# S5's result turned on chip, and b's gates as two units of seven block products behind w_proj_b

## The chip, the cores and the metric

The kernel runs on one core of one Trainium2 chip. The core's engines each have their own queue of instructions: TensorE (PE in the profile; PEld is its weight load) multiplies matrices, VectorE (DVE) and ScalarE (ACT) work element by element, GpSimd (POOL) does small jobs and starts DMAs that add to their target, and SyncE (SP) starts most of the other DMAs. The metric is the device time of one execution in microseconds. Before the change it is 876.34 us, the median of three runs (876.28 to 878.51).

## The reference

One layer of a hybrid encoder for 512 tokens of width 1024, in float32. What the change touches is the first part, the two mixers and their merge:

```python
n = rms_norm(h, mix_norm_g[i])
proj = n @ w_in[i]                       # 1024 x 4608, cut by columns:
xa = proj[..., :OFF_U]                   # 512: S5's input
zu = proj[..., OFF_U:OFF_V]              # 1024
zv = proj[..., OFF_V:OFF_GA]             # 1024
gate_a = jax.nn.sigmoid(proj[..., OFF_GA:OFF_GB])    # 1024
gate_b = jax.nn.sigmoid(proj[..., OFF_GB:])          # 1024
ya = s5_branch(xa, ...)       # two scans, then y = gelu(y); y * sigmoid(y @ w_glu)
yb = sgu_branch(zu, zv, ...)  # gelu(zu) * (mixed, normalized gelu(zv))
merged = gate_a * (ya @ w_proj_a[i]) + gate_b * (yb @ w_proj_b[i])
h = h + merged @ w_out[i]
```

Behind it come a cross-attention to a memory of 256 rows (w_q, w_k, w_v, w_xo), a SwiGLU FFN of width 2816 (w_gate, w_up, w_down) and a last norm. The output is 512 x 1024.

## The kernel before, in words

**Matmuls.** Every float32 operand is split into a high part (a cast on ScalarE) and a low part (source minus high part, on VectorE); `split` (L83, its two instructions L85 and L86) does both. A product is then three matmuls, hi·hi, hi·lo and lo·hi (`mm3`, L347, the matmul L350). Activations of the mixers stand with channels on the partitions and tokens along the free dimension, so a weight block is the stationary operand and 512 tokens stream: `feat` (L352) takes 256 output columns at a time into two PSUM banks (`pf0`, `pf1`), through `feat_block` for each 512 rows of the weight, and then calls an evacuation for each 128 columns.

**Weights.** All weight blocks are in one list, `plan`, in the order of their use; each entry has loads (how many entries ahead each is to be issued) and a function that splits the loaded block. `next_w` (L322) hands out the next block, issues the loads that are due and splits up to two blocks ahead (`LOADS, SPLITS = 3, 2`). The raw blocks share three buffers. A consumer must call `next_w` in the order of the plan, which checks it. `plan_sums` (L252) hangs 32 more jobs on chosen entries: sums of blocks of w_q and w_down that later stages use (`qsum`, `dsum`, in DRAM), a copy on SyncE's queue and an accumulating DMA on GpSimd's (L268), which read the blocks of weights long before their stage.

**Seven products.** The query projection, and the FFN, compute a 2 x 2 x 2 block product with seven block products in place of eight (the Strassen-Winograd form): `product` (L1361, matmul L1370) multiplies a 512 x 256 weight block by 256 tokens, 24 matmuls of 128 x 256. Operands of some products are sums of weight blocks, or of quarters of the token matrix; the results are added in PSUM, or by ScalarE and VectorE.

**S5 on the side.** S5's work is a generator (`s5_program`, L992) that `tick` advances between the blocks of the main stream, with `later` for steps that wait for others. Its 32 groups are done in four octets. For each octet `s5_kernels` (L786) computes a small convolution kernel, spills it to DRAM (`kd`, L843 and L844 on GpSimd's queue) and loads it back eight times shifted (`tt`, L851, also GpSimd); `s5_outputs` (L942) copies the states (`ss`, L952 and L953 on ScalarE), multiplies (`py`, 48 matmuls, L966), applies gelu (L972), turns the result in four 128 x 128 transposes (`pyt`, L978), copies it (L982) and stores it to DRAM (`yd`, eight DMAs on SyncE's and ScalarE's queues). Instructions under `in_order` keep the program's order on their engine.

**Around the change.** The main stream runs: v's first half, S5's input, v's second half, a's gates (stored to DRAM, `gad`), sv, u (`zu_evac`, into `yb_hi` and `yb_lo`, in the slots E and D), and then for each 256 columns b's gates (from xn, evacuated by a sigmoid into `part`, L1155) and w_proj_b (from yb, multiplied onto `part` by VectorE, L1158). After that S5's pool is closed and a pool `merge` takes its memory: S5's result comes back from `yd` into `ygt`, is split into `yg_hi` and `yg_lo`, goes through w_glu (`glu_evac`, L1179), and w_proj_a and the merge follow (`pa_evac`, L1198), then w_out. Of the profile's stages, b's gates and w_proj_b run from about 211 to 307 us, w_glu starts at 307.6 us.

Of the kernel before, what the change touches and what calls it, by code (L numbers as in the profile page):

```python
# [17 lines left out]
P = 128  # L18
# [21 lines left out]
Q = 8  # L40
# [12 lines left out]
def hybrid_layer_kernel(  # L53
# [168 lines left out]

    def plan_units(units, down):
# [86 lines left out]
    for i in range(4):  # L310
# [7 lines left out]
    plan_sums([(5 + 3 * i, 3) for i in range(12)] + [(40 + 2 * i, 2) for i in range(8)] +  # L318
              [(79 + 3 * i, 3) for i in range(3)] + [(116 + 5 * i, 4) for i in range(9)])
# [282 lines left out]
    yd = [dp.tile([GO * C, Q, NCH], F32, name=f"yd{o}") for o in range(NO)]  # L602
# [26 lines left out]
    def s5_setup():  # L629
# [23 lines left out]
        raw_c = s5p.tile([P, 2, G, C], F32, name="raw_c")  # L653
# [94 lines left out]
        zr = s5p.tile([P, G, C], F32, name="bbr")  # L748
        zi = s5p.tile([P, G, C], F32, name="bbi")
# [192 lines left out]
    def s5_outputs(o):  # L942
# [13 lines left out]
        yt = tt.rearrange("p (i r) c -> p i r c", i=2)  # L956

        def mix_():
            ps = aux("py", (P, GO // 2, P))
            for r in range(GO // 2):  # L960
                for k in range(3):
                    for j in range(2):
                        g = 2 * r + j
                        a = (u[:, o * GO + g, :], ss[0][:, g, :], ss[1][:, g, :])[k]
                        b = (tt[:, g, :], lc(e_re, g), lc(e_im, g))[k]
                        in_order(nc.tensor.matmul(ps[64 * j:64 * j + 64, r, :], a, b, start=r == k == 0, stop=k == 2,  # L966
                                                  tile_position=(0, 64 * j), skip_group_check=True))
            later(0.5, lambda: squash(ps))

        def squash(ps):  # L970

            nc.scalar.activation(yt[:, 0], ps, AF.Gelu_apprx_tanh)  # L972
            later(1, back)

        def back():
            ps = aux("pyt", (P, GO // 2, P))
            for r in range(GO // 2):
                nc.tensor.transpose(ps[:, r, :], yt[:, 0, r, :], ident)  # L978
# [175 lines left out]
    def gb_evac(m, j, ps):  # L1154
        nc.scalar.activation(part[:, m - OFF_GB // P, :], ps, AF.Sigmoid)  # L1155

    def pb_evac(m, j, ps):
        nc.vector.tensor_tensor(part[:, m, :], ps, part[:, m, :], ALU.mult)  # L1158
# [20 lines left out]
    def glu_evac(m, j, ps):  # L1179
# [4 lines left out]
                                ygt[:, m, :].rearrange("p (l n) -> p l n", l=Q), ALU.mult)  # L1184
# [100 lines left out]
    K0, K1, T0, T1 = slice(0, 4), slice(4, 8), slice(0, 256), slice(256, 512)  # L1285
# [75 lines left out]
    def product(ps, u, q, start, ops):  # L1361

        hi, lo = next_w(u[0], u[1], q)
        for j in range(2):
            cs = slice(j * P, (j + 1) * P)
            for k in range(4):
                a = (hi[:, k, cs], lo[:, k, cs])
                b = (ops[q][0][:, k, :], ops[q][1][:, k, :])
                for i, (x, y) in enumerate(((0, 0), (0, 1), (1, 0))):
                    nc.tensor.matmul(ps[:, j, :], a[x], b[y], start=start and j == k == i == 0,  # L1370
                                     stop=k == 3 and i == 2, skip_group_check=True)
        tick(2.7)

    def unit_bank(name):
        return bank(name).rearrange("p (j t) -> p j t", j=2)

# [7 lines left out]

    def kept(x, name):
        t = np_.tile([P, 2, 256], F32, tag="ev", name=name, bufs=2)
        nc.scalar.copy(t, x)
        return t

    def minus(x, t):  # L1390
        nc.vector.tensor_tensor(t, x, t, ALU.subtract)
        return t

# [381 lines left out]
```

## Time and profile before

| what | before |
|---|---|
| median of 3 runs | 876.34 us |
| the profiled execution | 877.18 us |
| its span | 875.4 us |
| TensorE busy | 862.9 us (99%), 5753 matmuls |
| VectorE busy | 617.4 us (71%) |
| ScalarE busy | 464.1 us (53%) |
| GpSimd busy | 104.9 us (12%) |
| HBM read, written | 146.60 MB, 38.24 MB |
| the chain that ended last | TensorE 93%, VectorE 5%, ScalarE 1% |

The span is the time from the first to the last instruction of the profiled execution; the execution's own time has a little around it. A row of instructions on the timeline has start, duration, engine, line, operation, output<-inputs and shape; what stands in brackets at its end is how long the engine was idle before it, and what released it. Matmuls are pipelined, so a matmul's duration (some 0.39 us for 128 x 512) is longer than the step from its start to the next one's. A row of a stretch gives the busy time of each engine in it, the number of instructions, the granted clock of TensorE, and the share and rate of the DMA engines. In DMA groups the last number is the time from issue to landing.

### The profile page before, as it was taken

How to read it: one execution, taken by the hardware profiler on the slowest of the kernel's cores; microseconds unless marked ns; L12 is line 12 of the kernel's file. 1: busy time of each engine (PE TensorE's matmuls, PEld its weight loads, DVE VectorE, ACT ScalarE, POOL GpSimd, SP SyncE). 2: the span in 40 equal slices, each digit the busy share in tenths (PEclk: the TensorE clock that was granted, in tenths of full speed). 3: DMA queues.
4: the chain of work that ended last, by engine and by line, in shares of the span. 5: the costliest groups of instructions: out<-in, count | busy, mean ns of one | idle time of the engine just before them, and what ended most of it. 6: DMA issues, size and time to landing. Idle time of an engine off the chain costs nothing.

```text
span 875.4 us, 14560 instructions
## 1 busy us (share of the span) xinstructions
PE 862.9 (99%) x5753; PEld 759.9 (87%) x5753; DVE 617.4 (71%) x867; ACT 464.1 (53%) x684; POOL 104.9 (12%) x154
## 2 busy tenths in 40 slices
PE   9999999999999999999999999999999999999996
PEld 6787888887888888889899878999999999888875
DVE  5699679968313258669657646767877768898875
ACT  5544875277434234557557444645545454556663
POOL 1001065103311100110000001001111110000000
PEclk9999999999999999999999999999999999999998
DMA  8358369943759946825687144547788963256672
GB/s 260 112 148 249 78 200 257 248 125 107 205 133 278 263 134 211 270 88 174 196 262 218 52 137 128 145 129 187 178 217 212 233 165 79 82 166 198 194 249 87
DMA packets 112134, 154.34 MB, mean 176 GB/s; under 512 B 13545, under 2 KB 78593, under 8 KB 112002
## 3 DMA queue, kind: packets, MB, share of 16 engines
q1 hardware_dynamic: 93042, 128.27, 45.2%
q0 software_dynamic: 16432, 24.09, 16.6%
q10 hardware_dynamic: 2592, 1.05, 0.5%
q8 instruction: 45, 0.74, 0.3%
q14 instruction: 23, 0.19, 0.1%
HBM read 146.60 MB, written 38.24 MB: 211 GB/s over the span
## 4 chain that ended last, share of the span: by engine, by line
PE 93%; DVE 5%; ACT 1%; issue 1%; POOL 0%; POOLq 0%
PE pf L350 29%; PE pt L350 17%; PE px L1370 12%; PE dx L350 7%; PE pq L1370 6%; PE dq L350 3%; PE pv L1370 3%; PE qx L1370 2%; PE dv L350 2%; PE ptr L511 1%; PE py L966 1%; PE po L350 1%; PE qq L1370 1%; DVE wlo L86 1%; PE pz L902 1%; PE pw L883 1%
## 5 line engine op out<-in xcount | busy, mean ns | idle before, releaser
L86 DVE TENSOR_TENSOR wlo<-wraw,whi 128x1024 fp32r<-128x1024 f32 (+1 forms) x139 | 165.0, 1187 | 110.2 <-ACT whi L85 106.9
L85 ACT CAST whi<-wraw 128x1024 fp32r<-128x1024 f32 (+1 forms) x139 | 142.3, 1024 | 168.2 <-PE pf L350 60.1
L350 PE MATMUL pf<-xn,whi 128*128 128x512 f32 x448 | 140.6, 393 | 0.0
L350 PEld LDWEIGHTS pf<-xn,whi 128*128 128x128 f32 x448 | 83.4, 188 | 17.9 <-issue 1.1
L350 PE MATMUL pf<-xn,wlo 128*128 128x512 f32 x224 | 87.7, 391 | 0.0
L1370 PE MATMUL px<-fn,whi 128*128 128x256 f32 x480 | 83.3, 277 | 0.0
L1370 PEld LDWEIGHTS px<-fn,whi 128*128 128x128 f32 x480 | 72.4, 188 | 0.3 <-ACT u L1630 0.2
L85 ACT CAST whi<-b 128x1024 fp32r<-128x1024 f32 x40 | 42.1, 1053 | 50.5 <-PE px L1370 27.1
L86 DVE TENSOR_TENSOR wlo<-b,whi 128x1024 fp32r<-128x1024 f32 x40 | 49.0, 1224 | 28.0 <-ACT whi L85 28.0
L1370 PE MATMUL px<-fn,wlo 128*128 128x256 f32 x240 | 66.5, 277 | 0.0
L350 PE MATMUL dx<-whi,s 128*128 128x512 f32 x170 | 53.9, 392 | 1.4 <-ACT whi L85 1.0
L1370 PE MATMUL pq<-s,whi 128*128 128x256 f32 x320 | 55.1, 277 | 0.0
L86 DVE TENSOR_TENSOR wlo<-t,whi 128x1024 fp32r<-128x1024 f32 x30 | 36.7, 1225 | 20.1 <-ACT whi L85 20.1
L85 ACT CAST whi<-t 128x1024 fp32r<-128x1024 f32 x30 | 31.6, 1052 | 36.0 <-PE pv L1370 12.6
L350 PEld LDWEIGHTS pf<-xn,wlo 128*128 128x128 f32 x224 | 42.1, 188 | 8.6
L1370 PEld LDWEIGHTS pq<-s,whi 128*128 128x128 f32 x320 | 48.3, 188 | 0.1
L1370 PEld LDWEIGHTS px<-fn,wlo 128*128 128x128 f32 x240 | 45.1, 188 | 0.0
L1370 PE MATMUL pq<-s,wlo 128*128 128x256 f32 x160 | 44.3, 277 | 0.0
L350 PE MATMUL pt<-whi,xn 128*128 128x512 f32 x128 | 42.4, 404 | 0.0
L350 PEld LDWEIGHTS dx<-whi,s 128*128 128x128 f32 x170 | 31.7, 188 | 8.4 <-ACT whi L85 1.2
L350 PE MATMUL dx<-wlo,s 128*128 128x512 f32 x85 | 33.1, 390 | 0.0
L1370 PEld LDWEIGHTS pq<-s,wlo 128*128 128x128 f32 x160 | 30.1, 188 | 0.0
(436 smaller groups left out, 2132.1 us busy)
## 6 DMA issues: line engine op xcount, KB each, us to landing
wraw<-in_w_in_dram SPq DMA_DIRECT2D x36, 512.0 KB, 5.2
dsum<-in_w_down_dram SPq DMA_DIRECT2D x20, 512.0 KB, 6.9
wraw<-dsum SPq DMA_DIRECT2D x20, 512.0 KB, 4.1
b<-in_w_gate_dram SPq DMA_DIRECT2D x15, 512.0 KB, 4.1
b<-in_w_up_dram SPq DMA_DIRECT2D x15, 512.0 KB, 3.9
wraw<-in_w_down_dram SPq DMA_DIRECT2D x15, 512.0 KB, 3.8
dsum<-in_w_down_dram POOLq DMA_DIRECT2D x10, 512.0 KB, 7.6
dsum<-dsum POOLq DMA_DIRECT2D x10, 512.0 KB, 7.7
```

The costliest lines, as they stand in the source:

```text
L85: hi = nc.scalar.copy(dst_hi, src)
L86: lo = nc.vector.tensor_tensor(dst_lo, src, dst_hi.bitcast(F32), ALU.subtract)
L350: nc.tensor.matmul(ps, a[x], b[y], start=start and i == 0, stop=stop and i == 2, skip_group_check=free)
L511: tr = nc.tensor.transpose(ps[:, j, :], src[:, k * P:(k + 1) * P], ident)
L883: nc.tensor.transpose(ps[:, j, :], wt[:, 4 * hf + j, :], ident)
L902: in_order(nc.tensor.matmul(ps[hf, g, :], wt[:, g, hf], x, start=g == 0, stop=True, tile_position=(0, 64 * j), skip_group_check=True))
L966: in_order(nc.tensor.matmul(ps[64 * j:64 * j + 64, r, :], a, b, start=r == k == 0, stop=k == 2, tile_position=(0, 64 * j), skip_group_chec ...
L1370: nc.tensor.matmul(ps[:, j, :], a[x], b[y], start=start and j == k == i == 0, stop=k == 3 and i == 2, skip_group_check=True)
```

## The change

S5's result no longer goes through DRAM. Its four transposes become sixteen 64 x 64 matmuls with an identity per octet, which leave the result in PSUM with the layout that w_glu reads; one copy brings it into `ygt` (two tiles of the "gain" buffers). The DMAs to and from `yd` are gone.

w_proj_b now runs through as a whole first, evacuated by a plain copy on ScalarE. b's gates come after it, as two units of 512 columns with seven block products each, in the overlapping order `ORDER`. Their token quarters are the rows of xn itself, left in place; three sums of quarters are made on VectorE during w_proj_b (`gate_sum`), and split into the slots D and E once yb is done with. Weight sums are made by accumulating DMAs on GpSimd and on VectorE, in a tile of S5's pool. The results go through a sigmoid on ScalarE and are multiplied onto `part` on VectorE. `product`, `unit_bank`, `kept` and `minus` are the functions that the query projection had; they only move up. The places of the jobs of `plan_sums` are adapted to the shorter plan. After the change mm3's matmul is L390 and product's L1210.

```diff
+    GATES = [(w_in, OFF_GB), (w_in, OFF_GB + 512)]
+    ORDER = ((1, 0), (2, 0), (5, 0), (6, 0), (1, 1), (7, 0), (2, 1), (5, 1), (6, 1), (3, 0), (7, 1), (4, 0), (4, 1), (3, 1))
+    def plan_gates():
+        kh = KD // 2
+        for q, i in ORDER:
...
+            def make(q=q, i=i, b=b, got=got):
+                t, b11 = (gate_place[0](2 * i + j) for j in range(2))
+                if q in (2, 3):
+                    return halves(got.pop("raw"))
+                ops = halves(b11 if q in (1, 7) else t)
+                if q == 5:
+                    nc.vector.tensor_tensor(t, t, got.pop("raw"), ALU.add)
+                elif q == 6:
+                    nc.vector.tensor_tensor(b11, t, b11, ALU.subtract)
+                    nc.gpsimd.dma_start(t, b(1, 0), accum_op=ALU.add)
+                return ops
+            loads = {1: [(5, whole(2 * i + 1, b(0, 0)))], 2: [(LOADS, plain(b(1, 0)))],
+                     5: [(8, whole(2 * i, b(0, 0))),
+                         (6, lambda i=i, b=b: nc.gpsimd.dma_start(gate_place[0](2 * i), b(0, 1), accum_op=ALU.add)),
+                         (LOADS, plain(b(1, 1)))],
+                     3: [(LOADS, plain(b(1, 1)))]}
...
     for c0 in range(0, D, 256):
-        plan_feat(w_in, OFF_GB + c0, KD)
         plan_feat(w_proj_b, c0, KD)
+    plan_gates()
...
-    plan_sums([(5 + 3 * i, 3) for i in range(12)] + [(40 + 2 * i, 2) for i in range(8)] +
-              [(79 + 3 * i, 3) for i in range(3)] + [(116 + 5 * i, 4) for i in range(9)])
+    plan_sums([(5 + 3 * i, 3) for i in range(10)] + [(38, 5), (44, 5)] + [(50 + 2 * i, 2) for i in range(7)] +
+              [(85 + 3 * i, 3) for i in range(3)] + [(122 + 5 * i, 4) for i in range(10)])
...
-            nc.scalar.activation(yt[:, 0], ps, AF.Gelu_apprx_tanh)
+            nc.scalar.activation(yl.rearrange("p l (r c) -> p r l c", c=C), ps.rearrange("p r (l c) -> p r l c", c=C),
+                                 AF.Gelu_apprx_tanh)
             later(1, back)
 
         def back():
-            ps = aux("pyt", (P, GO // 2, P))
-            for r in range(GO // 2):
-                nc.tensor.transpose(ps[:, r, :], yt[:, 0, r, :], ident)
+            ps = aux("pyt", (P, Q, NCH))
+            for l in range(Q):
+                for j in range(2):
+                    hf = slice(64 * j, 64 * j + 64)
+                    in_order(nc.tensor.matmul(ps[hf, l, :], yl[hf, l, :], ident[hf, hf], start=l == 0, stop=True,
+                                              tile_position=(64 * j, 64 * j), skip_group_check=True))
             later(0.5, lambda: emit(ps))
 
         def emit(ps):
-            nc.scalar.copy(yt[:, 1], ps)
-            y = yt[:, 1].rearrange("p r (g n) -> p (r g) n", n=NCH)
-            ydo = yd[o].rearrange("(g c) l n -> l c g n", c=C)
-            for l in range(Q):
-                (nc.sync, nc.scalar)[l % 2].dma_start(ydo[l], y[C * l:C * l + C])
+            if o % 2 == 0:
+                ygt.append(np_.tile([P, 2, T], F32, tag="gain", name="ygt", bufs=2))
+            nc.scalar.copy(ygt[o // 2][:, o % 2, :], ps.rearrange("p l n -> p (l n)"))
...
-    def gb_evac(m, j, ps):
-        nc.scalar.activation(part[:, m - OFF_GB // P, :], ps, AF.Sigmoid)
-
     def pb_evac(m, j, ps):
-        nc.vector.tensor_tensor(part[:, m, :], ps, part[:, m, :], ALU.mult)
-
-    for c0 in range(0, D, 256):
-        feat(w_in, OFF_GB + c0, xn, KD, gb_evac)
+        nc.scalar.copy(part[:, m, :], ps)
...
+    gate_place[0] = gate_tile
+    for n, c0 in enumerate(range(0, D, 256)):
         feat(w_proj_b, c0, yb, KD, pb_evac)
+        gate_sum(n)
+
+    gd, ge = (slot(tag, (P, KD * T), F32R, "gs" + tag.lower()) for tag in "DE")
+    at_ = lambda t, i: t[:, i:i + 1024].rearrange("p (k n) -> p k n", k=4)
+    gops[5], gops[6] = halves_at(gd, 4, 256, APART), halves_at(ge, 4, 256, APART)
+    gops[3] = (at_(gd, 2176 + APART[0]), at_(ge, 2048 + APART[1]))
+    split(*gops[5], gsum[1])
+    split(*gops[6], gsum[2])
+    onto(gsum[2], gops[2], ALU.add)
+    split(*gops[3], gsum[2])
...
+    def gate_put(i, f, ts, src):
+        m = 4 * i + 2 * f
+        V.tensor_tensor(part[:, m:m + 2, ts], part[:, m:m + 2, ts], src, ALU.mult)
...
+    def gate_step(q, i):
+        u = GATES[i]
+        if q == 1:
+            gx[i], gv[i] = unit_bank("gx"), unit_bank("gv")
+            product(gx[i], u, 1, True, gops)
+            nc.scalar.copy(gv[i], gx[i])
+        elif q == 2:
+            product(gv[i], u, 2, False, gops)
+            gate_put(i, 0, T0, sigmoid(gv[i]))
+        elif q == 5:
+            gq[i] = unit_bank("gq") if i == 0 else aux("gq").rearrange("p (j t) -> p j t", j=2)
+            product(gq[i], u, 5, True, gops)
+        elif q == 6:
+            product(gx[i], u, 6, False, gops)
+            nc.scalar.copy(u2s[i], gx[i])
+        elif q == 7:
+            product(gx[i], u, 7, False, gops)
+            u3 = minus(gq[i], kept(gx[i], "u3"))
+            gate_put(i, 1, T1, sigmoid(u3, u3))
+        elif q == 4:
+            product(gx[i], u, 4, False, gops)
+            gate_put(i, 0, T1, sigmoid(gx[i]))
+        else:
+            product(gq[i], u, 3, False, gops)
+            u2 = minus(gq[i], u2s[i])
+            gate_put(i, 1, T0, sigmoid(u2, u2))
+
+    for q, i in ORDER:
+        gate_step(q, i)
     finish_side()
     s5.close()
...
-    ygt = mgp.tile([P, 4, T], F32, name="ygt")
     for m in range(4):
-        nc.sync.dma_start(ygt[:, m, :], yd[m].rearrange("p l n -> p (l n)"))
-        split(yg_hi[:, m, :], yg_lo[:, m, :], ygt[:, m, :])
+        split(yg_hi[:, m, :], yg_lo[:, m, :], ygt[m // 2][:, m % 2, :])
```

More of the change, by code (lines that the diff above doesn't have):

```diff
@@ L601, in hybrid_layer_kernel @@
     ud = dp.tile([SW, Q, NCH], F32, name="ud")
-    yd = [dp.tile([GO * C, Q, NCH], F32, name=f"yd{o}") for o in range(NO)]
+    ygt = []
     st = {}
@@ L747, in s5_setup @@
         yield 1.5
[L748 to L749 removed]
+        zr = s5p.tile([P, G, C], F32, tag="bbr", name="bbr")
+        zi = s5p.tile([P, G, C], F32, tag="bbi", name="bbi")
         w = s5p.tile([P, 2, G, C], F32, tag="etmp", name="bbw")
@@ new lines, in product @@
+    def product(ps, u, q, start, ops):
+        hi, lo = next_w(u[0], u[1], q)
+        for j in range(2):
+            cs = slice(j * P, (j + 1) * P)
+            for k in range(4):
+                a = (hi[:, k, cs], lo[:, k, cs])
+                b = (ops[q][0][:, k, :], ops[q][1][:, k, :])
+                for i, (x, y) in enumerate(((0, 0), (0, 1), (1, 0))):
+                    nc.tensor.matmul(ps[:, j, :], a[x], b[y], start=start and j == k == i == 0,
+                                     stop=k == 3 and i == 2, skip_group_check=True)
+        tick(2.7)
@@ L1359, in values @@
             split(ot_hi[:, 2 * hd + dt_, :], ot_lo[:, 2 * hd + dt_, :], ps)
[L1361 to L1375, printed above, removed]
     def query_product(ps, n, q, start=False):
@@ L1383, in seed @@
         return v
[L1385 to L1392, printed above, removed]
     pts = {}
```

69 lines of the change are left out of this document (64 added, 5 removed).

## The prediction

> **What bounds the kernel now.** I read the page's busy shares, then its chain, then busy time by stretch, then single matmuls on the timeline.
>
> ```profile
> span 875.4 us, 14560 instructions
> PE 862.9 (99%) x5753; PEld 759.9 (87%) x5753; DVE 617.4 (71%) x867; ACT 464.1 (53%) x684; POOL 104.9 (12%) x154
> PE 93%; DVE 5%; ACT 1%; issue 1%; POOL 0%; POOLq 0%
> ```
>
> ```profile
> core 0: us, PE busy (x) PEld busy (x) DVE busy (x) ACT busy (x) POOL busy (x), PEclk, DMA share, GB/s
> 211.30:259.50 48.20, 48.20 (x343) 39.41 (x342) 16.63 (x19) 23.64 (x25) 17.99 (x34) 1.00 0.62 159
> 259.50:307.40 47.90, 47.90 (x215) 39.73 (x214) 16.78 (x18) 14.55 (x18) 5.61 (x6) 1.00 0.91 258
> 307.40:330.00 22.60, 22.60 (x101) 18.73 (x100) 12.91 (x15) 8.68 (x12) 1.17 (x1) 1.00 0.42 116
> 486.00:490.00 4.00, 3.41 (x25) 2.87 (x24) 4.00 (x16) 4.00 (x17) 0.00 (x0) 1.00 0.26 91
> ```
>
> TensorE carries 93% of the chain. The changed stage is the first two stretches (b's gates and w_proj_b, with S5's last octets between) and the third is w_glu and w_proj_a behind it: TensorE is busy in every microsecond of them. So whatever shortens TensorE's stream there shortens the kernel, one for one, and whatever makes TensorE wait lengthens it. VectorE and ScalarE are under half busy in the first two: there the order of their work counts, not the amount. For the same reason the 32 stores and four loads of S5's round trip through DRAM, which go, earn nothing: no wait of TensorE in these rows hangs on them.
>
> **The pace of TensorE.** Start to start, on the timeline (start, duration, engine, line):
>
> ```profile
> 224.48 0.40 PE L350 MATMUL pf<-yb_hi,whi 128*128 128x512 f32 x1
> 233.79 0.39 PE L350 MATMUL pf<-yb_hi,wlo 128*128 128x512 f32 x1
> 436.62 0.39 PE L1370 MATMUL qq<-hse,whi 128*128 128x256 f32 x2
> 439.34 0.39 PE L1370 MATMUL qv<-hn,whi 128*128 128x256 f32 x2
> 556.42 0.40 PE L1370 MATMUL pv<-fn,whi 128*128 128x256 f32 x2
> 558.54 0.63 PE L350 MATMUL pf<-fn,s 128*128 128x256 f32 x4
> ```
>
> Between the first two rows lie 41 intervals: 9.31 us, 0.2271 us for a 128x512 matmul. Between the third and the fourth lie the 24 matmuls of one block product: 2.72 us, 0.1133 us for a 128x256 one, half of the wide one. The last two show a second pace: 18 narrow matmuls in 2.12 us, 0.1178 us.
>
> **Term 1, the gates' matmuls.** Before: two halves of 512 columns, each 8 token-and-weight blocks, together 192 matmuls of 128x512: 192 x 0.2271 = 43.6 us. After: 2 units x 7 products x 24 = 336 of 128x256: 336 x 0.1133 = 38.1 us. That is -5.5 us. At the slower pace it would be 39.6 us and -4.0. I take -5.5, since the new units stand in one unbroken run, as the query products of the third row do, with all of S5's small matmuls ahead of them. w_proj_b's own 192 matmuls and S5's products stay the same in number.
>
> **What one wait costs.**
>
> ```profile
> 505.20 0.39 PE L350 MATMUL po<-p_hi,vt 128*128 128x512 f32 x1
> 506.26 0.50 PE L350 MATMUL pt<-whi,ot_hi 128*128 128x512 f32 x1 [0.68 <-ACT ot_hi L85]
> 506.60 0.40 PE L350 MATMUL pt<-wlo,ot_hi 128*128 128x512 f32 x1
> 307.35 0.39 PE L350 MATMUL pf<-yb_hi,wlo 128*128 128x512 f32 x1
> 307.58 0.39 PE L350 MATMUL pf<-yg_hi,whi 128*128 128x512 f32 x1
> ```
>
> From 505.20 to 506.60 is 1.40 us where two steps take 0.45: 0.95 us lost for 0.68 us shown idle. So a wait costs its idle time and about 0.26 us. The last two rows are the place where the gates' stage ends now: w_glu follows w_proj_b at the ordinary step, without a wait.
>
> The operations of ScalarE (ACT) and VectorE (DVE) that the waits below are made of:
>
> ```profile
> L85 ACT CAST whi<-b 128x1024 fp32r<-128x1024 f32 x40 | 42.1, 1053 | 50.5 <-PE px L1370 27.1
> L86 DVE TENSOR_TENSOR wlo<-b,whi 128x1024 fp32r<-128x1024 f32 x40 | 49.0, 1224 | 28.0 <-ACT whi L85 28.0
> L1155 ACT ACTIVATE part<-pf x8: 590/596/601, 222.2 to 297.6; 128x512 f32<-128x512 f32 x8
> L1158 DVE TENSOR_TENSOR part<-pf,part x8: 683/692/692, 232.9 to 307.8; 128x512 f32<-128x512 f32 x8
> L85 ACT CAST yg_hi<-ygt x4: 620/620/622, 273.8 to 279.9; 128x512 fp32r<-128x512 f32 x4
> L1382 ACT COPY qv<-qx x2: 578/578/578, 437.7 to 448.5; 128x512 f32<-128x512 f32 x2
> ```
>
> **Term 2, into the gates.** The token sums of products 5 and 6 go into the slots that held yb, so their splits (ScalarE hi, VectorE lo) can begin only when w_proj_b's last matmul has read yb. TensorE meanwhile has product 1 of the first unit: 24 x 0.1133 = 2.72 us. ScalarE in its order: sum hi 1.05, weight hi 1.05, the last copy of w_proj_b 0.58, second sum hi 1.05, the seed copy of a product 0.58. VectorE: sum lo 1.22 from 1.08 on, then the weight's lo 1.22: done at 3.5. Product 5 has issued its two hi matmuls by 2.9 and waits for that: 0.6 us. Product 6 then needs five VectorE passes in a row: the second sum's lo, which can start at 3.8 when ScalarE has cast its hi, a weight addition, an addition to the next token sum, a weight subtraction and the weight's lo, each 1.22: done at 9.9. TensorE, with products 5 and 2 behind it and the first 0.6 us lost, is there at 9.3: 0.6 more. Those two waits are the term: +1.2 us, from +0.3 (they overlap with TensorE's queue and only one restart is paid) to +1.9 (both with 0.26 us). Behind them each operand is ready 0.2 to 1 us early by the same adding up; if one more is late it is by less than the 1.22 us of one VectorE pass.
>
> **Term 3, out of the gates.** Now nothing can follow at once: w_glu's operand yg lies in memory that S5's pool gives back, and its first ScalarE cast waits for the last gate multiply, which reads a tile of that pool. From T, the end of the last product: VectorE's subtraction 0.69 (the multiply's 692 ns row is the same shape), ScalarE's sigmoid 0.60. But ScalarE has begun the cast of a w_proj_a block at T - 0.1 (1.05, so the sigmoid starts at about T + 0.97), and VectorE has its lo half (1.22) ahead of the gate multiply: that runs from T + 0.97 to 2.2. The multiply ends at T + 2.9, yg's first cast (0.62) at T + 3.6. With 0.26 us of restart: +3.9 us. Without the block's split between, 0.69 + 0.60 + 0.69 + 0.62 = 2.6 and 0.26: 2.9 is the lower end; 5.1, one more VectorE pass ahead, the upper. The cover that this wait takes away is w_proj_b: its 192 matmuls stood there, and they have gone ahead of the gates. After it, w_glu's remaining operands follow at 0.62 and 0.69 us each, against 12 matmuls (2.7 us) per block, so nothing else is late; w_glu's own weights are split before T.
>
> **Term 4, turning S5's result.**
>
> ```profile
> 259.51 0.60 PE L978 MATMUL pyt<-ident,tt 128*128 128x128 f32 x4
> 259.87 0.47 PE L350 MATMUL pf<-yb_hi,whi 128*128 128x512 f32 x1
> 91.24 2.08 PE L902 MATMUL pz<-u,wsx 128*64 128x64 f32 x64
> 93.25 0.44 PE L883 MATMUL pw<-ident,inx 128*128 128x128 f32 x2
> ```
>
> Four full transposes (0.36 us) become sixteen 64x64 matmuls per octet. The nearest row is pz, 64 of 64 columns in 2.01 us, 0.031 each: 0.50 us per octet. +0.14 x 4 = +0.5 us; ends -0.4 (two halves of the array at once) and +1.2. The copy out of PSUM stays on ScalarE; the 16 DMA issues on its queue and 16 on SyncE's go, at no gain for TensorE, which waited for neither.
>
> **Term 5, GpSimd's queue.** Four accumulating gate loads join it, among kd's stores and tt's loads for S5, and the w_down sums are placed anew.
>
> ```profile
> 236.28 0.51 POOL L844 DMA_DIRECT2D kd<-ks x1 [2.89 <-DMA dsum<-in_w_down_dram]
> 236.79 1.20 POOL L268 DMA_DIRECT2D dsum<-in_w_down_dram  x1
> 238.87 0.56 POOL L851 DMA_DIRECT2D tt<-kd  x1 [0.87 <-PE pf L350]
> 243.32 0.53 POOL L851 DMA_DIRECT2D tt<-kd  x1 [0.56 <-DMA dsum<-in_w_down_dram]
> 251.62 0.44 PE L966 MATMUL py<-tt,u 128*64 128x128 f32 x4
> tt<-kd POOLq DMA_DIRECT2D x16, 64.0 KB, 4.2
> dsum<-in_w_down_dram POOLq DMA_DIRECT2D x2, 512.0 KB, 6.8
> ```
>
> A transfer here already waits for an accumulate eight places before it to land (the 2.89 and 0.56). Octet 3's last tt load issues at 243.3, lands at some 247.5, and TensorE reads it at 251.6: 4 us of slack. Two accumulates more ahead of it, each 1.2 us to issue and 6.8 to land, one of them waited for, take 2.4 to 8 of those 4 us while w_proj_b's stream moves the reading some 2 us later. By adding up, it is ready 1 us before it is read, plus or minus 3. I take 0, with ends 0 and +4. The sums' SyncE halves only wait for free tiles, and the second unit's last accumulate lands 28.3 to 31.8 us behind the gates' start where it is needed by 30.4: 0, at most +1.4.
>
> **Sum.** -5.5 + 1.2 + 3.9 + 0.5 + 0 = +0.1 us. The profiled execution took 877.18 us (span 875.4), 0.84 above the median of 876.34 and within the runs shown (876.28 to 878.51). Forecast: 877.3 us, no change within 0.3% (2.6 us, which is also about the least that this measurement can tell from none). Terms 1 to 3 are both sure in sign and close to each other in size, so the outcome lies with the small ones.
>
> **Rivals.**
> - Faster. The two entry waits vanish behind TensorE's queue (0.3) and the exit costs its lower end (2.9), with term 4 at nothing: -5.5 + 0.3 + 2.9 - 0.4 = -2.7, and 0.6 less where w_proj_a's cast, now ahead of the sigmoid, runs earlier than T - 0.1: 873.9 us. For it: ScalarE and VectorE are under half busy in the first two stretches. Against: the operations in each chain are in a fixed order, and each of them needs the one before.
> - Slower by S5's octet. GpSimd's queue makes tt late, and TensorE, whose order is fixed, waits ahead of py: 3 to 4 us, 880.8. For it: the 2.89 us wait above; against: 4 us of slack now. It decides when tt's last load lands over 1 us later than I add up.
> - Slower by pace. After the waits the gates and the matmuls behind go at 0.1178 and 0.2333 instead: 336 x 0.0045 = 1.5 us, and as much in w_glu, w_proj_a and w_out: 880.3. For it: the 556.42 rows; against: the query products.
> - Slower by the clock. The exit would be TensorE's longest wait since its start; if it came back at half speed for about as long as it had waited, fifteen wide matmuls (3.4 us) would take 0.227 us more each: +3.4, 880.7. Against: the granted clock is 1.00 in every row above, the one with 0.59 us idle too; no row has an idle time of 3 us. The Trainium skill (TensorE: Matmul & The Clock Gate, "What's actually happening") has the clock halved after a whole idle window of some 3.4 us, of free-running phase. By that rule a 3.6 us idle stretch would seldom hold a whole window, so the sum would mostly stay at 877.3; an estimate from the page, one such window spent at half speed, would add 1.7 us and make it 879.0. The rows above agree as far as they go, with waits under 1 us at a granted clock of 1.00; no run so far shows a wait that long.
>
> **How the numbers follow.** The sum as it stands: 0.42, with 875.0 to 879.6 as its own range. Faster: 0.20. S5's octet 0.18, pace 0.12, clock 0.08. That gives faster 0.20, same 0.42, slower 0.38. The range for 8 in 10 goes from 872.8 (terms 2 to 4 at their low ends, -2.7, and the exit's 2.9 reduced to its last three operations, 1.9 us, with w_proj_a's split and the subtraction out of the way, -1.0 and -0.7) to 881.8 (octet case with part of the pace).
>
> **What would show it.** In the new profile: 336 narrow L1210 matmuls at 0.1133 in one run; two idles of about 0.6 us in its first 10 us, released by VectorE's lo; one idle of about 3.6 us ahead of the first pf<-yg_hi, released by ScalarE's cast of yg_hi; sixteen pyt matmuls in 0.5 us; py without a wait. I am wrong if the idle ahead of w_glu is under 2 us, if py shows a wait over 1 us on tt, if the granted clock drops behind the exit, or if a wait appears in w_proj_a or later.

## The result, and the profile after

The changed kernel takes 892.67 us against 876.34 us before: 1.8% longer, ratio 1.0179, 95% interval 1.016 to 1.0199. The prediction said 877.3 us, with 872.8 to 881.8 as its range.

The page of the changed kernel, busy time and chain:

```profile
span 891.9 us, 15074 instructions
PE 867.3 (97%) x6009; PEld 769.6 (86%) x6009; DVE 647.3 (73%) x895; ACT 476.6 (53%) x704; POOL 110.5 (12%) x158
PE 87%; DMA 5%; DVE 4%; issue 2%; ACT 2%; SPq 0%; POOLq 0%; POOL 0%; DVEq 0%; ACTq 0%
```

TensorE is busy 4.4 us longer though it has less arithmetic, and the chain now has 5% of DMA, which it did not have at all. To see how much belongs to the changed stretch, I take two marks that both kernels have: one of S5's products (`py`) shortly ahead of the first new instruction, and w_out's first matmul. Before, then after:

```profile
192.62 0.55 PE L966 MATMUL py<-e,ss 128*64 128x128 f32 x6
340.22 0.39 PE L350 MATMUL pt<-whi,mg_hi 128*128 128x512 f32 x1
```

```profile
193.24 0.44 PE L1006 MATMUL py<-e,ss 128*64 128x128 f32 x4
356.32 0.39 PE L390 MATMUL pt<-whi,mg_hi 128*128 128x512 f32 x1
```

147.60 us have become 163.08: 15.5 of the 16.3 us lie between these marks. All runs below are read by this stretch. Of what is in it, the waits come first (from the changed kernel's list of TensorE's waits: who waited, for whom, total, times, longest), and then stretches around the two long ones (busy time by engine, granted clock, DMA):

```profile
PE py L1006 <- DMA tt<-kd: 4.6, 1, 4.6
PE pf L390 <- ACT yg_hi L85: 3.6, 1, 3.6
PE pk L858 <- DVE e L847: 1.1, 1, 1.1
...
243.00:251.00 8.00, 5.45 (x49) 5.28 (x50) 4.29 (x4) 0.21 (x1) 4.73 (x8) 0.57 1.01 224
251.00:256.00 5.00, 5.00 (x24) 3.84 (x24) 1.11 (x1) 1.44 (x2) 2.92 (x6) 1.00 0.21 49
316.00:319.40 3.40, 0.00 (x0) 0.00 (x0) 2.41 (x4) 2.00 (x4) 0.14 (x1) 0.90 0.50 160
319.40:326.00 6.60, 6.59 (x17) 5.17 (x17) 2.48 (x4) 1.51 (x3) 1.16 (x1) 0.54 0.91 317
```

Both waits are followed by a stretch in which the granted clock is at half: 0.57 and 0.54 as means, 0.50 microsecond by microsecond. So a wait is paid twice, as idle time and as slow matmuls behind it. The first sits ahead of S5's third octet, the second between the gates and w_glu. GpSimd's timeline ahead of the first one:

```profile
223.42 1.35 POOL L258 DMA_DIRECT2D gw<-in_w_in_dram  x1 [8.15 <-DMA gw<-in_w_in_dram]
226.26 1.18 POOL L308 DMA_DIRECT2D dsum<-in_w_down_dram  x1 [1.49 <-DMA dsum<-in_w_down_dram]
226.99 1.02 POOL L891 DMA_DIRECT2D tt<-kd  x1
229.16 1.30 POOL L258 DMA_DIRECT2D gw<-in_w_in_dram  x1 [1.15 <-DMA gw<-in_w_in_dram]
237.99 1.04 POOL L891 DMA_DIRECT2D tt<-kd  x2 [2.91 <-DMA dsum<-in_w_down_dram]
```

The first gate accumulate (L258) waits 8.15 us for the block that it adds to, and the loads of `tt` stand behind it; the last two of them issue from 238.0 us on, where `py` wants its data at 240.8. The small matmuls of the turning, on TensorE's timeline:

```profile
201.47 1.15 PE L1022 MATMUL pyt<-ident,tt 64*64 64x64 f32 x32
203.70 0.43 PE L858 MATMUL pk<-e,bd 128*32 128x128 f32 x8 [1.09 <-DVE e L847]
272.00 1.15 PE L1022 MATMUL pyt<-ident,tt 64*64 64x64 f32 x32
273.08 0.50 PE L390 MATMUL pf<-yb_lo,whi 128*128 128x512 f32 x1
```

An octet's turning occupies 1.08 us where four transposes took 0.36: sixteen matmuls of the program stand as 32 in the trace. And the gates themselves:

```profile
275.71 0.40 PE L1210 MATMUL gx<-xn,whi 128*128 128x256 f32 x2
299.32 0.28 PE L1210 MATMUL gx<-gse,wlo 128*128 128x256 f32 x1
301.81 0.28 PE L1210 MATMUL gq<-gsd,wlo 128*128 128x256 f32 x1
304.31 0.39 PE L1210 MATMUL gx<-xn,whi 128*128 128x256 f32 x2
312.93 0.29 PE L1210 MATMUL gq<-gsd,whi 128*128 128x256 f32 x1
315.56 0.28 PE L1210 MATMUL gq<-gsd,wlo 128*128 128x256 f32 x1
319.41 1.65 PE L390 MATMUL pf<-yg_hi,whi 128*128 128x512 f32 x3 [3.58 <-ACT yg_hi L85]
```

From 275.71 to 315.67 are 39.96 us for the 336 matmuls: 3.6 less than 43.6, not 5.5. From 304.31, 72 matmuls that stream xn take 8.62 us, 0.1197 each; from 299.32, 22 that stream a split sum take 2.49, 0.1132 each.

### The profile page after: what moved, and what is told of

Read it like the earlier page. It is cut to its first block, busy times and chain, and to the rows that moved or that the text cites. A ratio compares the mean times of both kernels' runs of the same rounds, so it can differ in the third digit from the quotient of the medians.

```text
span 891.9 us, 15074 instructions
## 1 busy us (share of the span) xinstructions
PE 867.3 (97%) x6009; PEld 769.6 (86%) x6009; DVE 647.3 (73%) x895; ACT 476.6 (53%) x704; POOL 110.5 (12%) x158
## 4 chain that ended last, share of the span: by engine, by line
PE 87%; DMA 5%; DVE 4%; issue 2%; ACT 2%; SPq 0%; POOLq 0%; POOL 0%; DVEq 0%; ACTq 0%
PE pf L390 20%; PE pt L390 17%; PE px L1210 12%; PE dx L390 6%; PE pq L1210 6%; PE dq L390 3%; PE pv L1210 3%; PE qx L1210 2%; DMA dsum<-in_w_down_dram 2%; PE gx L1210 2%; PE dv L390 2%; DVE wlo L86 1%; PE po L390 1%; PE qq L1210 1%; PE py L1006 1%
## 5 line engine op out<-in xcount | busy, mean ns | idle before, releaser
L86 DVE TENSOR_TENSOR wlo<-wraw,whi 128x1024 fp32r<-128x1024 f32 (+1 forms) x135 | 160.0, 1186 | 93.3 <-ACT whi L85 93.0
L85 ACT CAST whi<-wraw 128x1024 fp32r<-128x1024 f32 (+1 forms) x135 | 138.0, 1023 | 141.8 <-PE pf L390 39.3
L390 PE MATMUL pf<-xn,whi 128*128 128x512 f32 x320 | 100.2, 393 | 0.0
L1210 PE MATMUL px<-fn,whi 128*128 128x256 f32 x480 | 83.3, 276 | 0.0
L1210 PEld LDWEIGHTS px<-fn,whi 128*128 128x128 f32 x480 | 72.6, 188 | 0.3 <-ACT u L1763 0.2
L390 PEld LDWEIGHTS pf<-xn,whi 128*128 128x128 f32 x320 | 59.6, 188 | 12.8 <-issue 0.7
L1210 PE MATMUL px<-fn,wlo 128*128 128x256 f32 x240 | 66.4, 277 | 0.0
L390 PE MATMUL pf<-xn,wlo 128*128 128x512 f32 x160 | 62.6, 392 | 0.0
L390 PE MATMUL dx<-whi,s 128*128 128x512 f32 x170 | 53.9, 391 | 1.4 <-ACT whi L85 1.0
L1210 PE MATMUL pq<-s,whi 128*128 128x256 f32 x320 | 55.2, 276 | 0.0
L1210 PEld LDWEIGHTS pq<-s,whi 128*128 128x128 f32 x320 | 48.4, 188 | 0.1
L1210 PEld LDWEIGHTS px<-fn,wlo 128*128 128x128 f32 x240 | 45.1, 188 | 0.0
L390 PE MATMUL pt<-whi,xn 128*128 128x512 f32 x128 | 43.7, 416 | 0.7 <-ACT xn L85 0.7
L1210 PE MATMUL pq<-s,wlo 128*128 128x256 f32 x160 | 44.2, 277 | 0.0
L390 PEld LDWEIGHTS dx<-whi,s 128*128 128x128 f32 x170 | 31.7, 188 | 8.4 <-ACT whi L85 1.2
L390 PEld LDWEIGHTS pf<-xn,wlo 128*128 128x128 f32 x160 | 30.1, 188 | 6.3 <-issue 0.2
L390 PE MATMUL dx<-wlo,s 128*128 128x512 f32 x85 | 33.2, 391 | 0.1
L1210 PEld LDWEIGHTS pq<-s,wlo 128*128 128x128 f32 x160 | 30.1, 188 | 0.0
```

Of the source, the lines that this page charges most:

```text
L85: hi = nc.scalar.copy(dst_hi, src)
L86: lo = nc.vector.tensor_tensor(dst_lo, src, dst_hi.bitcast(F32), ALU.subtract)
L390: nc.tensor.matmul(ps, a[x], b[y], start=start and i == 0, stop=stop and i == 2, skip_group_check=free)
```

## The experiments

The theory from the traces has four parts: GpSimd's queue (the first wait and its half clock), the way out of the gates (the second), the turning, and the pace of the products on xn. Each was first taken away or done alone, then the remedies were put together. "Stretch" is the time between the two marks; the ratios are to the kernel before, run beside it.

**The clock behind the exit.** An addition of unread matmuls:

```diff
     for q, i in ORDER:
         gate_step(q, i)
+    p = aux("long")
+    for i in range(16):
+        in_order(nc.tensor.matmul(p, xn_hi[:, 0, 0:P], xn_hi[:, 0, :], start=True, stop=True))
     finish_side()
```

> The changed kernel with sixteen 128x512 matmuls on xn, whose result nobody reads, between the last gate product and w_glu. Changed kernel 892.7 us. Theory (the wait of 3.58 us ahead of w_glu also halves the clock behind it): the sixteen take 16 x 0.227 = 3.6 us in the place of the wait, the granted clock stays at 1.00, and the first fifteen w_glu matmuls go at 0.227 and not 0.43: 2.7 us less, 890.0. Rival (the slow matmuls there wait for yg's splits or for DMA traffic): they stay at 0.43, 892.7.

Measured: 889.56 us, ratio 1.0132 (1.0117 to 1.0148); stretch 159.67, 3.4 us less. TensorE's timeline at the place, and the stretch behind it:

```profile
314.16 3.80 PE L1327 MATMUL long<-xn 128*128 128x512 f32 x16
317.91 0.96 PE L390 MATMUL pf<-yg_hi,whi 128*128 128x512 f32 x3
317.90:325.00 7.10, 7.10 (x32) 5.90 (x32) 2.49 (x4) 1.53 (x3) 1.11 (x1) 1.00 0.88 308
```

With the same data coming at the same time, w_glu runs at a clock of 1.00: 32 matmuls in 7.1 us, where the changed kernel has 17 in 6.6. The slow matmuls were neither yg's splits nor the DMA traffic (0.88 here too), and the half clock costs some 3 us at this wait: w_glu's 48 matmuls take 11.0 us instead of 13.8. Most of the rest of the 3.4 us lies at the first wait, whose half clock lasted 3.4 us in this run and 6.8 in the changed kernel's.

**The w_down sums in GpSimd's queue.**

```diff
-    plan_sums([(5 + 3 * i, 3) for i in range(10)] + [(38, 5), (44, 5)] + [(50 + 2 * i, 2) for i in range(7)] +
+    plan_sums([(5 + 3 * i, 3) for i in range(8)] + [(50 + 2 * i, 2) for i in range(7)] + [(64 + 4 * i, 3) for i in range(4)] +
```

> The changed kernel with the four w_down sums whose accumulating DMAs stand in GpSimd's queue among S5's last octets placed some 20 to 30 blocks later. Theory (those sums hold up the tt loads, TensorE waits 4.56 us ahead of py, and comes back at half clock): the wait and the half clock go, 4.56 + 0.26 + 2.4 = 7.2 us less, 885.5. Rival (the gate's own accumulating loads hold tt up as well): py still waits some 2 to 4 us and the time falls by under 3 us, to 890 or more.

Measured: 890.7 us, ratio 1.0140 (1.0123 to 1.0157); stretch 160.95, 2.1 us less. The rival held: a wait of 3.5 us stays, with its half clock. Of the 2.1 us only 1.1 are this wait; 1.3 are the exit, where the half clock lasted 3.4 us in this run and not 6.8. GpSimd's timeline shows why the wait stays, since the gate accumulates wait as before and `tt`'s last load comes at 234.4:

```profile
221.35 1.35 POOL L258 DMA_DIRECT2D gw<-in_w_in_dram  x1 [7.91 <-DMA gw<-in_w_in_dram]
225.79 1.30 POOL L258 DMA_DIRECT2D gw<-in_w_in_dram  x1 [3.10 <-DMA gw<-in_w_in_dram]
234.44 0.53 POOL L891 DMA_DIRECT2D tt<-kd  x1 [2.79 <-DMA gw<-in_w_in_dram]
```

The list of waits names a store of `kd` for this wait; but GpSimd's next issue, at 239.45, is released by `tt`'s landing, and `py` starts at 239.47. The order of TensorE's work changes with the edit, too: `py` stands 14 wide matmuls (3.2 us) further ahead in it, and 16 in the two runs below that take the gate sums off GpSimd's queue, so it asks for `tt` earlier.

**yg split within the gates.** yg, ya and a's gates go into dead tiles of S5's pool (`Pair` holds two of them):

```diff
-    for q, i in ORDER:
...
+    for n, (q, i) in enumerate(ORDER):
         gate_step(q, i)
-    finish_side()
-    s5.close()
...
+        if n == 10:
+            finish_side()
+            yg_hi, yg_lo = s5p.tile([P, 4, T], F32R, tag="u", name="yg_hi"), Pair("tt", "yg_lo")
+            for m in range(4):
+                split(yg_hi[:, m, :], yg_lo[:, m, :], ygt[m // 2][:, m % 2, :])
+    ya_hi, ya_lo = Pair("e0", "ya_hi"), Pair("e1", "ya_lo")
...
     for c0 in range(0, D, 256):
         feat(w_proj_a, c0, (ya_hi, ya_lo), 4, pa_evac)
-    mgx.close()
+    s5.close()
```

> The changed kernel with yg, ya and a's gates in dead tiles of S5's pool, so that the pool is given back after w_proj_a and yg is split behind the eleventh of the fourteen gate products. Theory (the wait ahead of w_glu is the chain subtraction, sigmoid, multiply and cast, and nothing else): no wait there, no half clock: 3.58 + 0.26 + 2.7 = 6.5 us less, 886.1. Rival (ScalarE and VectorE have no room for yg's eight passes of 0.6 to 0.7 us within the gates): the waits move into the last gate products, and less than half of it is gained, 889.5 or more.

Measured: 885.28 us, ratio 1.0082 (1.0062 to 1.0102); stretch 155.59, 7.5 us less. The exit of the gates on its timeline:

```profile
315.44 0.28 PE L1210 MATMUL gq<-gsd,wlo 128*128 128x256 f32 x1
315.55 0.40 PE L390 MATMUL pf<-yg_hi,whi 128*128 128x512 f32 x1
```

The last product and w_glu follow each other at the ordinary step. The wait, its restart and its half clock were the chain of subtraction, sigmoid, multiply and cast behind a pool that was given back late; the eight passes for yg find room among the last products. With it goes a wait of 0.54 us in w_proj_a, on VectorE's `mg`.

**Where xn lies.**

```diff
-    xn_hi, xn_lo = token_slot("xn")
+    xn_hi, xn_lo = token_slot("xn", APART)
```

> The changed kernel with xn's two halves shifted by 48 and 112 elements in their slot, as the query's and the FFN's operands are. Theory (the gate products that stream xn go at 0.1196 and not 0.1133 because of where xn lies): 8 of 14 products, 192 x 0.0063 = 1.2 us less, 891.5, and gx<-xn at 0.1133. Rival (the slower pace comes from what runs before): no change, 892.7, xn products at 0.1196.

Measured: 892.53 us, ratio 1.0165 (1.0150 to 1.0180), so no gain that can be told from the changed kernel's 1.0179. The timeline of the three last xn products:

```profile
303.77 0.50 PE L1210 MATMUL gx<-xn,whi 128*128 128x256 f32 x3
311.93 0.28 PE L1210 MATMUL gq<-gsd,whi 128*128 128x256 f32 x1
```

They do go at 8.16 us for 72, 0.1133 each, so the place of the operand mattered here; but the first product on xn went at 0.1178 in the same run. What the gates win the wide matmuls on xn lose: ahead of the first mark, the longest unbroken run (96 of pf<-xn) takes 22.57 us from its start to the next work's instead of 21.94, and all runs of 15 or more 2.6 us more together. The stretch is 160.57, 2.5 us less, of which the gates are 1.1; 0.8 are a shorter wait ahead of `pk`, and 1.0 the first wait's half clock, which lasted 3.4 us in this run and not 6.8.

**The gate sums off GpSimd's queue.** A plain load and one addition on VectorE:

```diff
+                elif q == 1:
+                    nc.vector.tensor_tensor(t, t, got.pop("raw"), ALU.add)
...
-            loads = {1: [(5, whole(2 * i + 1, b(0, 0)))], 2: [(LOADS, plain(b(1, 0)))],
+            loads = {1: [(5, whole(2 * i + 1, b(0, 0))), (LOADS, plain(b(0, 1)))], 2: [(LOADS, plain(b(1, 0)))],
                      5: [(8, whole(2 * i, b(0, 0))),
-                         (6, lambda i=i, b=b: nc.gpsimd.dma_start(gate_place[0](2 * i), b(0, 1), accum_op=ALU.add)),
```

> The changed kernel with the first sum of each gate unit (two weight blocks for product 5) made by a plain load and one VectorE addition, in place of the accumulating DMA on GpSimd's queue; the w_down sums stay where they are. Changed kernel 892.7 us. Theory (the two gate accumulates wait in GpSimd's queue for whole blocks to land, and tt's loads stand behind them): the first tt load of octet 2 issues some 8 us earlier, py waits under 1 us and the half clock behind it goes, 5 to 7 us less, 886 to 888. Rival (the w_down sum between kd's stores and tt's loads is enough to hold tt): py still waits 2 us or more, above 889.

Measured: 886.82 us, ratio 1.0099 (1.0082 to 1.0116); stretch 157.10, 6.0 us less. The wait ahead of `py` falls to 1.3 us (the profile names no releaser for it), and the clock stays at 1.00 there. That the first load of `tt` would issue some 8 us earlier did not come: it issues at 226.37, since a w_down sum now holds the queue, on GpSimd's timeline:

```profile
225.64 1.19 POOL L309 DMA_DIRECT2D dsum<-in_w_down_dram  x1 [11.16 <-DMA dsum<-in_w_down_dram]
226.37 4.14 POOL L892 DMA_DIRECT2D tt<-kd  x7
233.86 0.53 POOL L892 DMA_DIRECT2D tt<-kd  x1 [3.35 <-DMA dsum<-in_w_down_dram]
```

**Both off the queue.** The edits of the last run and of the one on the w_down sums together.

> The gate sums by VectorE and the four w_down sums placed later, together. Theory (these two are all that holds tt up): no wait ahead of py, 4.56 + 0.26 + 2.4 = 7.2 us less than the changed kernel, 885.5. Rival (kd's stores or the octet's own products are late too): a wait of over 1 us stays, above 887.

Measured: 887.28 us, ratio 1.0110 (1.0095 to 1.0125); stretch 155.98, 7.1 us less, and `py` follows without a wait. On GpSimd's timeline `tt`'s first load is 11 us earlier than in the two runs where one of the causes is still there:

```profile
215.27 4.22 POOL L892 DMA_DIRECT2D tt<-kd  x8 [1.53 <-DMA kd<-ks]
```

The stretch agrees with the 7.2 expected. In the whole time the 1.1 us gained over the last run do not show: behind the second mark the profiled execution is 3.6 us longer than the last run's, with four new waits of 0.3 to 0.8 us at the query projection and ahead of it. That the sums placed there bring them is not shown; "all four" below has the sums in the same places and none of these waits.

**The turning alone**, in the kernel before: only the diff's part from `yl` to `emit`, and `ygt`.

> The kernel before with S5's result turned on chip, and nothing else of the change: b's gates and w_proj_b as they were. Theory of the traces (the sixteen 64x64 matmuls of an octet take 1.07 us where four transposes took 0.36, and the third octet's kernel products then wait 1.1 us for VectorE): 4 x 0.71 + 1.1 + 0.26 = 4.2 us more than before; without that wait, which depends on the order around it, 2.8. The prediction's term: 0.5 more. Rival (the DMAs saved give it back in less traffic): no change.

Measured: 880.2 us, ratio 1.0032 (1.0019 to 1.0045); stretch 151.64 against 147.60, 4.0 us more. Its timeline:

```profile
200.02 1.15 PE L982 MATMUL pyt<-ident,tt 64*64 64x64 f32 x32
202.28 0.42 PE L818 MATMUL pk<-e,bd 128*32 128x128 f32 x8 [1.11 <-DVE e L807]
```

4 x 0.71 + 1.1 + 0.26 = 4.2 was the theory's sum. The prediction's 0.5 falls, and so does the notion that fewer DMAs give it back.

**All four edits.**

> The changed kernel with all four edits: yg early, gate sums by VectorE, w_down sums later, xn shifted. If the losses add up: 892.7 - 6.5 (or the 7.4 measured for yg early) - 7.2 - 1.2 = 877 to 878, as long as the kernel before and up to 1 us more, with the turning's 4 us as what eats the gates' 5.5. Rival (they overlap, the DMA queues or VectorE become the limit): above 880.

Measured: 879.87 us, ratio 1.0028 (1.0017 to 1.0039); stretch 148.38. By the ratios 1.5 of the 1.8% are back; it is not as fast as before. The gates' timeline held a surprise:

```profile
296.81 0.40 PE L1211 MATMUL gx<-xn,whi 128*128 128x256 f32 x2
305.29 0.28 PE L1211 MATMUL gq<-gsd,whi 128*128 128x256 f32 x1
```

The same 72 xn products that took 8.16 us with xn shifted alone take 8.48 here, 0.1178 each, and so do all others of these gates. The place of xn is the same; so the pace has a second cause, which these runs do not name.

**The gates without the turning.** The edits for yg, the gate sums and the w_down sums, with the transposes and the way through `yd` as before:

```diff
...
+            for m in range(4):
+                if m % 2 == 0:
+                    ygt.append(np_.tile([P, 2, T], F32, tag="gain", name="ygt", bufs=2))
+                nc.sync.dma_start(ygt[m // 2][:, m % 2, :], yd[m].rearrange("p l n -> p (l n)"))
```

> The gates' seven products and w_proj_b ahead of them, with yg early, gate sums by VectorE and the w_down sums later, but S5's result turned by four transposes and taken through DRAM as before; xn where it was. Theory (the turning costs 3 to 4 us on TensorE's path, the gates gain 5.5 less 1.2 to 2 of pace and 0.5 of waits): 879.9 - 3.5 = 876.4 against 877.3 of before, up to 2 us faster than before. Rival (the loads from DRAM come too late for yg, or the sixteen-fold stores hold up weights): a wait ahead of w_glu, 879 or more.

Measured: 880.03 us, ratio 1.0033 (1.0018 to 1.0047); stretch 149.19. Neither expectation held: w_glu has its operands in time, but TensorE waits twice at the gates' entry. Its waits, and ScalarE's timeline there:

```profile
PE gx L1209 <- ACT whi L85: 1.7, 2, 1.6
PE gq L1209 <- ACT whi L85: 1.5, 1, 1.5
```

```profile
262.70 1.82 ACTq L1028 DMA_DIRECT2D yd<-tt  x4
264.56 0.59 ACT L1197 COPY part<-pf 128x512 f32<-128x512 f32 x1 [1.89 <-DMA yd<-tt]
```

The last octet's four stores on ScalarE's queue hold it for 1.9 us, while it has to make the gates' first splits; the run on the stores below tests this. In the kernel before, TensorE did not wait for ScalarE there. So the turning does bring something: not the DMAs' traffic, but ScalarE's queue.

**One wide matmul ahead of product 5**, in that kernel: `long_idle(xn_hi)` for the first unit.

> The same with one 128x512 matmul that nobody reads ahead of product 5 of the first unit. Theory (the pace of the narrow products is a state that one wide matmul or a wait sets back): the gates go at 0.1133 where their operands allow it, 0.5 to 1.5 us less than without it. Rival (the pace is fixed by where the operands lie): no change, or 0.2 us more.

Measured: 881.37 us, ratio 1.0034 (1.0021 to 1.0048); stretch 149.77. The rival held: every product behind it has the pace that it had without (72 of gx<-xn in 8.62 us). What sets the pace is not set back by a wide matmul.

**The shift in that kernel.**

> The kernel of the first of these three with xn shifted by 48 and 112 elements. Theory (the shift speeds the gates' narrow products on xn by up to 1.2 us and slows the wide matmuls on xn of the stages ahead by about as much, as the run with the shift alone showed: octet 1's product began 1.2 us later there): no change within 0.5 us. Rival (only the gates are touched): 1.2 us less.

Measured: 883.02 us, ratio 1.0055 (1.0036 to 1.0075); stretch 149.61. No gain: a wait of 1.56 us at the entry is followed here by 3.4 us of half clock (granted clock 0.50 from 273 to 275), the shifted gates then go at 0.1178, and the wide matmuls on xn ahead of the first mark lose 2.6 us as in the other run with the shift, more than the 1.2 us expected. The mark comes at 194.21 instead of 191.40, but without the shift it lies anywhere from 191.36 to 193.35.

**The stores off ScalarE's queue.**

```diff
-                (nc.sync, nc.scalar)[l % 2].dma_start(ydo[l], y[C * l:C * l + C])
+                nc.sync.dma_start(ydo[l], y[C * l:C * l + C])
```

> The gates' seven products without the turning (the kernel of three runs ago: yg early, gate sums by VectorE, w_down sums later, S5's result through DRAM), with all eight stores of an octet on SyncE's queue, none on ScalarE's. Theory (the four stores of the last octet hold ScalarE up for 3.7 us just ahead of the gates, and TensorE waits 3.2 us for the weights' casts): the two waits of 1.5 us go, 880.0 - 3 = 877, as long as before or up to 1 us less. Rival (SyncE's queue is held up by twice as many stores and the weights' loads behind them are late): a wait on DMA appears, 879 or more.

Measured: 877.86 us against 878.75 beside it (medians), ratio 0.9997 (0.9985 to 1.0009, which covers the 0.9990 of the medians); stretch 145.75. The two waits are gone, and this version is as fast as the kernel before. Its gates, from their first matmul to w_glu's:

```profile
263.15 0.40 PE L1209 MATMUL gx<-xn,whi 128*128 128x256 f32 x2
304.16 0.40 PE L391 MATMUL pf<-yg_hi,whi 128*128 128x512 f32 x1
```

41.0 us instead of 43.6: that, less 0.7 us of other work in the stretch, is what the seven products are worth here. Of the 0.7, w_proj_a has 0.6: its 96 matmuls take 22.39 us, and as long in all other kernels with yg split early, against 21.76 before. ya lies elsewhere in these; that its place is the cause was not tested. No version measured beats the kernel before.

| kernel | ratio to before | stretch, us |
|---|---|---|
| before | 1 | 147.6 |
| changed | 1.0179 | 163.1 |
| w_down sums later | 1.0140 | 161.0 |
| xn shifted | 1.0165 | 160.6 |
| filler at the exit | 1.0132 | 159.7 |
| gate sums by VectorE | 1.0099 | 157.1 |
| both of GpSimd's causes away | 1.0110 | 156.0 |
| yg early | 1.0082 | 155.6 |
| turning alone | 1.0032 | 151.6 |
| all four | 1.0028 | 148.4 |
| gates only | 1.0033 | 149.2 |
| gates only, one wide matmul | 1.0034 | 149.8 |
| gates only, xn shifted | 1.0055 | 149.6 |
| gates only, stores on SyncE | 0.9997 | 145.8 |

Each stretch is of one profiled execution. Added up step by step from TensorE's timelines, the 15.5 us of the changed kernel are 9.8 of waits (4.56, 3.58, 1.09, and 0.54 in w_proj_a), 5.3 of matmuls at half clock, 2.9 of the turning's small matmuls and 0.8 in w_proj_a, less 3.3 in the gates and w_proj_b together. From the runs, GpSimd's queue 7.1 and the exit 7.5 add up: all four edits took 14.7 off. With the turning 4.0 and the gates -1.9 that makes 16.7, which is 1.2 too much. The excess lies in the turning: alone it costs 4.0, but between "all four" and the last run, which differ in it and in the shift, it is 2.6; `pk` waits 1.11 us in the one place and 0.31 in the other.

## Why the prediction was wrong, step by step

The forecast of no change was wrong, and the direction that came was one it had given 0.38, as several rivals; no single rival had the size. (It was counted from the profiled execution's 877.18 us, 0.84 above the median; that plays no part in a miss of 15.) Three of the prediction's four signs of being wrong came: `py` waited on `tt`, the clock dropped behind the exit, and TensorE waited in w_proj_a.

- *What bounds the kernel.* Right: TensorE's stream in that stage moves the end one for one. 15.5 of 16.3 us lie there.
- *Term 1, -5.5.* Sign right, size 3.6 in the changed kernel and 2.6 in the last run. The step that failed is the pace: I took 0.1133 from the query's products, whose operands lie at shifted offsets, for operands that the change leaves in place. xn's products go at 0.1197. With the shift they went at 0.1133 in one kernel and at 0.1178 in two, so the place is part of it and not all. The slower end I gave, -4.0, was nearer. The rival's paces, 0.1178 and 0.2333, did not come in the changed kernel.
- *Term 2, +1.2.* One wait of 0.20 us came, not two of 0.6. Passes back to back follow each other faster than their durations, as VectorE's timeline of the changed kernel shows:

```profile
276.76 1.23 DVE L86 TENSOR_TENSOR gsd<-x,gsd 128x1024 fp32r<-128x1024 f32 x1 [5.51 <-ACT gsd L85]
277.91 1.22 DVE L86 TENSOR_TENSOR wlo<-gw,whi 128x1024 fp32r<-128x1024 f32 x1
283.69 1.22 DVE L86 TENSOR_TENSOR wlo<-gw,whi 128x1024 fp32r<-128x1024 f32 x1
```

  A step is 1.15 us for a pass of 1.22, and with the gates' own pace slower TensorE came later too.
- *Term 3, +3.9.* The wait was 3.58 us by the chain that I wrote down, 3.6. What was missing was its consequence: with the half clock it cost 7.5 (yg early), some 2.8 of it slow matmuls in w_glu (13.8 us against 11.0 with the filler).
- *Term 4, +0.5.* 4.0 (turning alone). I took the 64 matmul records of pz for 64 matmuls of the program; but a plain float32 matmul stands twice in the trace, as pyt's 32 for sixteen show, and `py`'s 48 an octet, which are 24 in the program. The transposes stand once. So an octet costs 1.08 and not 0.50. And I looked for nothing behind it: the next kernel products (`pk`) come to stand right after it, 1.1 us ahead of VectorE.
- *Term 5, 0.* 7.1 (both off the queue). Here the step that failed is the most instructive: I counted issue and landing of the accumulates, and not what each of them waits for in the queue. The first stands 8.15 us until its own block has landed, and all of `tt` behind it; a w_down sum alone does the same, and only with both away does `tt` issue at 215.27 instead of 226 or later. I also placed the risk in the last octet, where there was no wait; it was the one before. The rival "slower by S5's octet" had the mechanism and the idle time, 880.8, and not the half clock.
- *The half clock.* I gave it 0.08 and only at the exit, since no row of before shows a wait over 1.1 us in this stage. In these runs every wait of TensorE from 3.5 to 4.8 us in the stretch, ten of them in seven kernels, was followed by a granted clock of 0.50. Of six waits of 1.3 to 1.6 us in the stretch (one in the run with the gate sums by VectorE, two in each of the gates without the turning and the same with the wide matmul, one in the one with the shift) one was, in the last of these: 0.50 for 3.4 us, from 272.5 to 275.9, behind a wait of 1.56 us that ended at 271.1. The clock's times in the traces suggest what decides. Its changes lie on a grid of 3.41 us (the two falls in the changed kernel's stretch are 22 such steps apart). In ten of the eleven falls in the stretches TensorE had been idle for 63% or more of the step just ahead; of the three steps of the stretch that were 46% idle, one was followed by a fall, and of those with less, none. The Trainium skill (TensorE: Matmul & The Clock Gate, "What's actually happening") halves the clock after an idle window of some 3.4 us and restores it after a busy one; I read the free-running window as seldom fitting into 3.6 us. The trace agrees with the window's length, and neither with a wholly idle one nor with my reading: with a mean of 0.80 from 243 to 244 us and of 0.85 from 318 to 319, the clock fell 2.6 and 2.9 us into the idle time. It stayed low for some 6.8 us at both. TensorE worked in 4.9 and 6.1 of these, so that it lost 2.4 and 3 us, not the 1.7 that I worked out.

What stays open: why the same products run at 0.1133 in one kernel and at 0.1178 in another with the operands in the same places, and why w_proj_a is slower in the kernels with yg split early.

## What to carry to other kernels

When an instruction joins an in-order queue, ask first what it waits for and how long, and then what stands behind it: an accumulating DMA whose target is still being loaded holds everything on its queue. A TensorE wait of 3.5 us or more (ten of ten here), and now and then a shorter one (one of six from 1.3 to 1.6 us; nothing between was measured), is to be priced twice, once as idle time and once as the matmuls that follow at half clock. A price per matmul taken from another stage may not hold where the operands lie otherwise, and has to be counted per matmul of the program and not per record.

## What the runs showed of the hardware that was not expected

Shifting the streamed operand by 48 and 112 elements took a run of 96 wide matmuls from 21.94 to 22.57 us in each of the three kernels that have it, and 72 narrow ones from 8.62 to 8.16 in one of them and to 8.48 in the other two. The half clock lasted 6.8 us seven times and 3.4 us four times: two steps of the clock's grid or one, behind the same wait of 3.6 us at the exit too. And in three runs, the changed kernel's among them, the clock fell without any wait: there at 35.4 us, for 3.4 us, behind two rows of eight small matmuls (`pbc`, 64x64), with TensorE busy in the whole step ahead. The same work ran at full clock in the other eleven runs.
